# Later bank sums, silus and gate products in a hand-ordered gate-and-up loop, and one ring of transposition banks

## The chip, the cores and the metric

The kernel runs on one core of one Trainium2 chip. The metric is the device time of one execution in microseconds, as the median of several runs. One further execution was recorded by the hardware profiler; all rows below come from it.

Five engines work side by side, each through its own queue in order: TensorE (PE in the rows; PEld is its weight load), VectorE (DVE), ScalarE (ACT), GpSimd (POOL) and SyncE (SP, which here issues transfers). They wait for each other through semaphores. Matmuls write into PSUM, eight banks of 128 x 512 float32; DVE and ACT read the banks.

## The reference

A decoder trunk of two layers for 256 positions and a width of 2048, in float32. Cut to what matters here:

```
x = x + mixer(rms_norm(x))          # layer 0: retention and short convolution; layer 1: differential attention
x = x + swiglu(rms_norm(x))         # both layers

def swiglu(h, w_gate, w_up, w_down):          # 2048 -> 5632 -> 2048
    return (jax.nn.silu(h @ w_gate) * (h @ w_up)) @ w_down
```

The change touches the product of `h` with `w_gate` and `w_up` and what makes the hidden values out of it.

## The kernel before, in words

Every float32 matmul is done as three in a reduced format: each operand is split into a high part (a cast by ACT) and a low part (the operand minus the high part, by DVE), and PE multiplies high by high, low by high and high by low (L272 to L274). The low part of the weights enters only with the third.

`gate_up` (L188) makes the hidden values of one feed-forward layer. The 5632 hidden columns are 11 pairs of 512 columns, a pair being the gate columns and the up columns of the same numbers. `ffn` (L620) runs them in three parts of 4, 4 and 3 pairs; after each part `out_proj` or an equal loop multiplies the part's hidden values by the rows of `w_down`. So within the parts one pair follows another in 3 + 3 + 2 places per layer.

The gate and up products of both halves of the 256 rows share work in the manner of Strassen: the 2048 contraction rows of a pair are four chunks of 512, of the kinds 7, 8, 7, 8. In a chunk of kind 7 seven weight operands (w11, w21, t2, t3, t4, t1, w22; t1 to t4 are sums of weight blocks) are each multiplied into one bank, six matmuls each; in a chunk of kind 8 four operands go into two banks each, twelve matmuls each. An operand with its matmuls is a slot: slots 0 to 6 are the first chunk of a pair, 7 to 10 the second, 11 to 17 the third, 18 to 21 the fourth. Seven banks are summed up over the pair: b1, b2, b6 and b4 (four banks of tag `mm`), b7 (tag `tpa`), and b3 and b5, which are one tile of two banks of tag `sc` with a single buffer. In a chunk of kind 7 the operands go, in the order above, to b1, b2, b6, b7, b4, b5 and b3.

The order of the instructions in `gate_up` is written by hand (`manual_schedule`, L305). In the loop over the slots, step i first prepares slot i+3 (`prepare`: the cast on ACT, the low part on DVE at L183, and in chunks of kind 7 a helper sum on DVE behind the low parts of w11, w21 and t2, at L242, L244 and L246), then issues the matmuls of slot i, then calls `gather(i)`. High and low parts have four buffers each, so the cast of slot i+3 waits until slot i-1 is done. `gather` acts at three slots of each pair:

- at slot 14 (t3 of the third chunk) b1 is copied twice by ACT and b6 and b7 are summed with it by DVE (L284 to L287);
- at slot 19 DVE adds b2 and b4 to them, the gate values (L290, L291), and ACT applies two silus (L293);
- at slot 21, the last, DVE adds b5 twice and b3 once, the up values (L296 to L298), and multiplies gates by ups (L300, twice). The result is handed to `splits`, which transposes it on PE through a bank of `tp_tile` and splits it into high and low parts. That job advances by one step at each slot of the second chunk of the next pair: a step that does nothing, one half of the rows, the other half.

Since every engine works in order, a DVE operation issued at slot 21 stands in front of the low part that is prepared one step later.

`tp_tile` (L73) gives a bank for transpositions: in turn one of tag `tpa` and one of `tpb`, and during `gate_up` only `tpb`, since b7 holds `tpa`.

Of the kernel before, what the change touches and what calls it, by code (L numbers as in the profile page):

```python
# [9 lines left out]
F32 = mybir.dt.float32  # L10
F32R = mybir.dt.float32r
AF = mybir.ActivationFunctionType
ALU = mybir.AluOpType
# [3 lines left out]
P = 128  # L17
D = 2048
S = 256
NT = S // P  # L20
KT = D // P
NB = 512
# [13 lines left out]
def decoder_trunk(ctx: ExitStack, tc: tile.TileContext, a: dict):  # L36
    nc = tc.nc
# [27 lines left out]
    work.begin("mix0", 4)  # L65
    ctx.callback(lambda: work.close.close())

    tp_both, tp_turn = [True], [0]

    def acc_tile(name):  # L70
        return psum.tile([P, NB], F32, tag="mm", name=name, bufs=4)

    def tp_tile(name):  # L73
        tp_turn[0] ^= 1
        tag = "tpa" if tp_turn[0] and tp_both[0] else "tpb"
        return psum.tile([P, NB], F32, tag=tag, name=name, bufs=1)


    ident = cpool.tile([P, P], F32, name="ident")
# [58 lines left out]
    jobs = deque()  # L138

    def step():  # L140
        while jobs:
            try:
                next(jobs[0])
                return
            except StopIteration:
                jobs.popleft()
# [41 lines left out]
    def gate_up(layer, wg, wu, st, r, p0, p1, hi, lo):  # L188

        kinds = st.kinds
        nc_ = len(kinds)
        last7 = max(c for c, kind in enumerate(kinds) if kind == 7)
        last8 = max(c for c, kind in enumerate(kinds) if kind == 8)
        chunks = [(b, c) for b in range(p0, p1) for c in range(nc_)]
        tiles, banks, sums, begun = {}, {}, {}, set()

        def load(n):
            if n >= len(chunks):
                return
            b, c = chunks[n]
            nm = f"f{layer}{b}_{c}"
            x, y = work.raw_tile(nm + "x"), work.raw_tile(nm + "y")
            k0 = c * KD * P
            cols = slice(b * NB, (b + 1) * NB)

            def rows(w, nk):  # L210
                return w[k0 : k0 + nk * P, cols].rearrange("(k p) n -> p k n", p=P)

            nc.sync.dma_start(y, rows(wu, KD))
            nc.sync.dma_start(x, rows(wg, KD))
            if kinds[c] == 7:
                nc.gpsimd.dma_start(y[:, 0:KC], rows(wg, KC), accum_op=ALU.add)  # L216
            tiles[n] = {"w11": x[:, 0:KC], "w21": x[:, KC:KD], "w12": y[:, 0:KC], "w22": y[:, KC:KD]}

        SEVEN = (
            ("w11", (("b1", "a11"),)), ("w21", (("b2", "a12"),)), ("t2", (("b6", "s2"),)), ("t3", (("b7", "s3"),)),  # L220
            ("t4", (("b4", "a22"),)), ("t1", (("b5", "s1"),)), ("w22", (("b3", "s4"),)),
        )
        EIGHT = (
            ("w11", (("b2", "a11"), ("b4", "a21"))), ("w21", (("b2", "a12"), ("b4", "a22"))),
            ("w12", (("b5", "a21"), ("b3", "d1"))), ("w22", (("b5", "a22"), ("b3", "d2"))),
        )
        slots = []
        for n, (b, c) in enumerate(chunks):
            for operand, products in SEVEN if kinds[c] == 7 else EIGHT:
                slots.append((n, b, c, operand, products))  # L230
        ready = {}

        def prepare(i):
            n, b, c, operand, _ = slots[i]
            w = tiles[n]
            nm = f"f{layer}{b}_{c}"
            where = {"t1": "w12", "t3": "w11", "t4": "w21"}.get(operand, operand)
            ready[i] = split_w(w[where], nm + operand)
            if kinds[c] == 7:
                if operand == "w11":  # L240
                    w["t2"] = work.tile([P, KC, NB], F32, tag="t2", name=nm + "t2", bufs=1)
                    nc.vector.tensor_tensor(w["t2"], w["w12"], w["w22"], ALU.add)  # L242
                elif operand == "w21":
                    nc.vector.tensor_tensor(w["w11"], w["t2"], w["w11"], ALU.subtract)  # L244
                elif operand == "t2":
                    nc.vector.tensor_tensor(w["w21"], w["t2"], w["w21"], ALU.add)  # L246
            if operand == "w22":
                load(n + 3)

        def get_banks(b):  # L250
            nm = f"f{layer}{b}_"
            for i in (1, 2, 6, 4):
                banks[b, f"b{i}"] = acc_tile(f"{nm}p{i}")
            banks[b, "b7"] = psum.tile([P, NB], F32, tag="tpa", name=nm + "p7", bufs=1)
            b35 = psum.tile([P, 2, NB], F32, tag="sc", name=nm + "p35")
            banks[b, "b3"], banks[b, "b5"] = b35[:, 0], b35[:, 1]

        def multiply(i):
            n, b, c, operand, products = slots[i]
            whi, wlo = ready.pop(i)  # L260
            a = st.blocks(c)
            if (b, "b1") not in banks:
                get_banks(b)
            for bank, act in products:
                ahi, alo = a[act]
                acc = banks[b, bank]
                last = (last7 if bank in ("b1", "b6", "b7") else nc_ - 1) == c
                last = last and (kinds[c] == 7 or operand in ("w21", "w22"))
                for j in range(KC):
                    first = (b, bank) not in begun  # L270
                    begun.add((b, bank))
                    nc.tensor.matmul(acc, lhsT=ahi[:, j], rhs=whi[:, j], start=first, stop=False)  # L272
                    nc.tensor.matmul(acc, lhsT=alo[:, j], rhs=whi[:, j], start=False, stop=False)  # L273
                    nc.tensor.matmul(acc, lhsT=ahi[:, j], rhs=wlo[:, j], start=False, stop=last and j == KC - 1)  # L274

        def gather(i):

            n, b, c, operand, _ = slots[i]
            nm = f"f{layer}{b}"
            if c == last7 and operand == "t3":  # L280
                u = work.tile([P, NT, NB], F32, tag="u", name=nm + "u", bufs=1)
                g = work.tile([P, NT, NB], F32, tag="gs", name=nm + "gs", bufs=1)
                sums[b] = u, g
                nc.scalar.copy(u[:, 0], banks[b, "b1"])  # L284
                nc.vector.tensor_tensor(u[:, 0], banks[b, "b6"], u[:, 0], ALU.subtract)
                nc.scalar.copy(g[:, 0], banks[b, "b1"])
                nc.vector.tensor_tensor(u[:, 1], banks[b, "b7"], u[:, 0], ALU.add)  # L287
            if c == nc_ - 1 and operand == "w21":
                u, g = sums[b]
                nc.vector.tensor_tensor(g[:, 0], banks[b, "b2"], g[:, 0], ALU.add)  # L290
                nc.vector.tensor_tensor(g[:, 1], banks[b, "b4"], u[:, 1], ALU.subtract)  # L291
                for t in range(NT):
                    nc.scalar.activation(g[:, t], g[:, t], AF.Silu, scale=r[:, t : t + 1])  # L293
            if c == nc_ - 1 and operand == "w22":
                u, g = sums[b]
                nc.vector.tensor_tensor(u[:, 1], banks[b, "b5"], u[:, 1], ALU.add)  # L296
                nc.vector.tensor_tensor(u[:, 0], banks[b, "b5"], u[:, 0], ALU.add)
                nc.vector.tensor_tensor(u[:, 0], banks[b, "b3"], u[:, 0], ALU.add)  # L298
                for t in (1, 0):
                    nc.vector.scalar_tensor_tensor(  # L300
                        g[:, t], u[:, t], r[:, t : t + 1], g[:, t], op0=ALU.mult, op1=ALU.mult
                    )
                return splits((g[:, 1], g[:, 0]), hi, lo, 4 * (b - p0), f"h{layer}{b}", (1, 0))

        with tc.manual_schedule():  # L305
            for n in range(3):
                load(n)
            for i in range(AHEAD):
                prepare(i)
            for i, (n, b, c, operand, _) in enumerate(slots):  # L310
                if i + AHEAD < len(slots):
                    prepare(i + AHEAD)
                multiply(i)
                job = gather(i)
                if job:
                    jobs.append(job)
                if kinds[c] == 8 and n % nc_ == 1:
                    step()

    def act_pair(nk, tag, name):  # L320
        hi = apool.tile([P, nk, S], F32R, tag=tag + "h", name=name + "_hi")
# [156 lines left out]
            yield  # L478
            transpose4(srcs[t], dst, t, f"{name}{t}")

    def splits(srcs, hi, lo, k0, name, order=range(NT)):
        for src, t in zip(srcs, order):
            yield
            split4(src, hi, lo, k0, t, f"{name}{t}")


    st = Stream("n0", 0)
# [132 lines left out]
    def ffn(layer, st, r, after):  # L620
        wg, wu, wd = a["ffn_w_gate"][layer], a["ffn_w_up"][layer], a["ffn_w_down"][layer]
        res = None
        for part, (p0, p1) in enumerate(((0, 4), (4, 8), (8, 11))):
            hi, lo = act_pair(KT, "act", f"h{layer}{part}")
            tp_both[0] = False
            gate_up(layer, wg, wu, st, r, p0, p1, hi, lo)
            tp_both[0] = True
            nk, row0 = 4 * (p1 - p0), p0 * NB
            if part < 2:
                out_proj(f"d{layer}{part}", wd, nk, hi, lo, 0, row0, stream=False)  # L630
# [15 lines left out]
    st, r = ffn(0, st, r, 16)  # L646
# [28 lines left out]
    for i in range(2):  # L675
        ct, sn = rtab[:, 2 * i], rtab[:, 2 * i + 1]
        g = gains[:, i]
# [190 lines left out]
```

## Time and profile before

| | |
|---|---|
| median of 3 runs | 2257.22 us (2255.91 to 2258.88) |
| the profiled execution | 2256.58 us, span 2254.8 us |
| mean granted TensorE clock | 0.994 of full speed |
| PE busy | 2195.8 us, 97% |
| DVE busy | 1628.6 us, 72% |
| ACT busy | 1151.4 us, 51% |
| POOL busy | 174.1 us, 8% |
| moved by DMA | 441.99 MB, 196 GB/s |

How to read the rows. The busy line gives for each engine its busy time, share of the span and number of instructions. The slices cut the span in 40; a digit is a share in tenths, 9 being 90% or more. A line of the waits reads: engine, tile and source line, what it waited for, then the total in us, the number of waits and the longest. A line of the timeline reads: start in us, duration in us, engine, source line, operation, output and input, shapes, how many in a row are merged (x2), and in brackets the time that the engine stood idle before it and what released it. A line of the windows reads: the stretch in us from the start of the span, its length, the busy time and instructions of each engine, the mean granted clock (PEclk), the busy share of the DMA engines and what they moved. Matmuls overlap in their pipeline: they last 0.39 us in the rows but start every 0.23 us.

### The profile page before, as it was taken

To read this page: it belongs to the slowest core of one execution; us is meant where nothing else is said; L and a number is where in the kernel's file an instruction comes from. 1 tells how busy PE (TensorE), PEld (TensorE's weight loads), DVE (VectorE), ACT (ScalarE), POOL (GpSimd) and SP (SyncE) were. 2 spreads that over 40 slices of the span, in tenths; PEclk is the share of its full clock that TensorE was granted. 3 is DMA by queue.
4 is the path that set the end of the run, shared out by engine and by line. 5 is a ranking of instruction groups with operands and counts; after the bars stand their busy time and mean duration, and the time that the engine had idled before them with its cause. 6 is when DMAs were issued, how large, how long until landed. Compare 5 with 4: busy or idle time off the path is not lost. (4 is left out here: it accounts for less than half of the span.)

```text
span 2254.8 us, 25858 instructions
## 1 busy us (share of the span) xinstructions
PE 2195.8 (97%) x9851; PEld 1801.7 (80%) x9851; DVE 1628.6 (72%) x1742; ACT 1151.4 (51%) x1362; POOL 174.1 (8%) x148
## 2 busy tenths in 40 slices
PE   9999999999999999999999999998999999999999
PEld 7888888777887778878888888787778877788777
DVE  5555567888568885787577787677885688857884
ACT  5444455555346553555555544455564455545552
POOL 1100000000000000000132233000000000000000
PEclk9999999999999999999999999999999999999999
DMA  8555566666577656766465555466665767656752
GB/s 284 171 182 187 187 224 193 199 188 222 189 212 213 207 205 197 222 178 224 139 195 167 185 168 187 168 183 204 200 203 200 223 192 227 198 193 210 213 206 94
DMA packets 224832, 441.99 MB, mean 196 GB/s; under 512 B 8044, under 2 KB 11588, under 8 KB 224580
## 3 DMA queue, kind: packets, MB, share of 16 engines
q1 hardware_dynamic: 209904, 414.34, 54.0%
q0 software_dynamic: 11968, 23.07, 6.4%
q10 hardware_dynamic: 2836, 2.93, 0.4%
q8 instruction: 77, 1.26, 0.2%
q14 instruction: 47, 0.39, 0.1%
HBM read 438.22 MB, written 2.10 MB: 195 GB/s over the span
## 5 line engine op out<-in xcount | busy, mean ns | idle before, releaser
L216 POOL DMA_DIRECT2D f_0y<-in_ffn_w_gate_dram x22 | 26.6, 1210 | 1034.3 <-issue 214.3
L272 PE MATMUL f_p<-f_1w_hi,n_hi 128*128 128x512 f32 x264 | 106.2, 402 | 0.0
L274 PE MATMUL f_p<-f_3w_lo,n_hi 128*128 128x512 f32 x264 | 103.7, 393 | 0.4 <-DVE f_3w_lo L183 0.4
L274 PE MATMUL f_p<-f_1w_lo,n_hi 128*128 128x512 f32 x264 | 103.6, 392 | 0.0
L273 PE MATMUL f_p<-f_3w_hi,n_lo 128*128 128x512 f32 x264 | 103.2, 391 | 0.0
L273 PE MATMUL f_p<-f_1w_hi,n_lo 128*128 128x512 f32 x264 | 103.0, 390 | 0.0
L272 PE MATMUL f_p<-f_3w_hi,n_hi 128*128 128x512 f32 x264 | 103.0, 390 | 0.0
L183 DVE TENSOR_TENSOR f_0w_lo<-f_0x,f_0w_hi 128x1024 fp32r<-128x1024 f32 x44 | 53.9, 1226 | 56.6 <-ACT f_0w_hi L181 56.4
L274 PE MATMUL f_p<-f_0t_lo,n_c_sh 128*128 128x512 f32 x132 | 55.5, 420 | 40.1 <-DVE f_0t_lo L183 40.1
L183 DVE TENSOR_TENSOR f_2w_lo<-f_2x,f_2w_hi 128x1024 fp32r<-128x1024 f32 x44 | 53.9, 1226 | 35.5 <-ACT f_2w_hi L181 35.5
L181 ACT CAST f_0t_hi<-f_0x 128x1024 fp32r<-128x1024 f32 x44 | 46.2, 1051 | 56.3 <-DVE f_0x L244 25.2
L181 ACT CAST f_1w_hi<-f_1x 128x1024 fp32r<-128x1024 f32 x44 | 46.2, 1050 | 53.3 <-PE f_p L273 53.3
L181 ACT CAST f_0w_hi<-f_0x 128x1024 fp32r<-128x1024 f32 x44 | 45.9, 1043 | 47.9 <-PE f_p L273 27.9
L181 ACT CAST f_2w_hi<-f_2x 128x1024 fp32r<-128x1024 f32 x44 | 46.2, 1050 | 44.2 <-PE f_p L273 32.3
L274 PEld LDWEIGHTS f_p<-f_0t_lo,n_c_sh 128*128 128x128 f32 x132 | 25.9, 196 | 52.8 <-DVE f_0t_lo L183 47.1
L166 DVE TENSOR_TENSOR d00o_lo<-d00o_raw,d00o_hi 128x1024 fp32r<-128x1024 f32 x32 | 39.2, 1226 | 38.3 <-ACT d00o_hi L164 38.3
L166 DVE TENSOR_TENSOR d11o_lo<-d11o_raw,d11o_hi 128x1024 fp32r<-128x1024 f32 x32 | 39.2, 1225 | 38.3 <-ACT d11o_hi L164 38.3
L166 DVE TENSOR_TENSOR d01o_lo<-d01o_raw,d01o_hi 128x1024 fp32r<-128x1024 f32 x32 | 39.2, 1225 | 38.3 <-ACT d01o_hi L164 38.3
L166 DVE TENSOR_TENSOR d10o_lo<-d10o_raw,d10o_hi 128x1024 fp32r<-128x1024 f32 x32 | 39.2, 1225 | 38.3 <-ACT d10o_hi L164 38.3
L181 ACT CAST f_2t_hi<-f_2x 128x1024 fp32r<-128x1024 f32 x44 | 46.3, 1051 | 35.6 <-PE f_p L273 25.2
L166 DVE TENSOR_TENSOR n1o_lo<-n1o_raw,n1o_hi 128x1024 fp32r<-128x1024 f32 x32 | 39.1, 1224 | 30.0 <-ACT n1o_hi L164 30.0
L164 ACT CAST d11o_hi<-d11o_raw 128x1024 fp32r<-128x1024 f32 x32 | 33.6, 1049 | 52.3 <-PE d11o_a L173 46.7
(710 smaller groups left out, 7310.7 us busy)
## 6 DMA issues: line engine op xcount, KB each, us to landing
f_0y<-in_ffn_w_up_dram SPq DMA_DIRECT2D x22, 1024.0 KB, 6.4
f_0x<-in_ffn_w_gate_dram SPq DMA_DIRECT2D x22, 1024.0 KB, 6.6
f_1y<-in_ffn_w_up_dram SPq DMA_DIRECT2D x22, 1024.0 KB, 5.2
f_1x<-in_ffn_w_gate_dram SPq DMA_DIRECT2D x22, 1024.0 KB, 5.2
f_2y<-in_ffn_w_up_dram SPq DMA_DIRECT2D x22, 1024.0 KB, 5.3
f_2x<-in_ffn_w_gate_dram SPq DMA_DIRECT2D x22, 1024.0 KB, 6.0
f_3y<-in_ffn_w_up_dram SPq DMA_DIRECT2D x22, 1024.0 KB, 5.2
f_3x<-in_ffn_w_gate_dram SPq DMA_DIRECT2D x22, 1024.0 KB, 6.1
```

The source lines that it names most:

```text
L164: nc.scalar.copy(whi, part)
L166: nc.vector.tensor_tensor(wlo, part, whi.bitcast(F32), ALU.subtract)
L181: nc.scalar.copy(whi, src)
L183: nc.vector.tensor_tensor(wlo, src, whi.bitcast(F32), ALU.subtract)
L216: nc.gpsimd.dma_start(y[:, 0:KC], rows(wg, KC), accum_op=ALU.add)
L272: nc.tensor.matmul(acc, lhsT=ahi[:, j], rhs=whi[:, j], start=first, stop=False)
L273: nc.tensor.matmul(acc, lhsT=alo[:, j], rhs=whi[:, j], start=False, stop=False)
L274: nc.tensor.matmul(acc, lhsT=ahi[:, j], rhs=wlo[:, j], start=False, stop=last and j == KC - 1)
```

## The change

The sums, copies, silus and products of `gather` are put into a table, `later`, under the slot after whose matmuls they are to be issued, and the loop issues them there; what is still in the table behind the last slot of a part is issued at once, in the same order. The copies of b1 go from slot 14 to 16, the sums of b6 and b7 from 14 to 18, the silus from 19 to 22 (slot 0 of the next pair), the sums of b5 and b3 from 21 to 24 (slot 2 of the next pair), the products from 21 to 29 (slot 7 of the next pair), and with them the hand-over to `splits`. The sums of b2 and b4 stay at 19. The two halves of the rows are multiplied and transposed in the order 0, 1 instead of 1, 0. `tp_tile` draws from one tag of two buffers everywhere, and b7 is drawn from it too.

```diff
-    tp_both, tp_turn = [True], [0]
     def tp_tile(name):
-        tp_turn[0] ^= 1
-        tag = "tpa" if tp_turn[0] and tp_both[0] else "tpb"
-        return psum.tile([P, NB], F32, tag=tag, name=name, bufs=1)
+        return psum.tile([P, NB], F32, tag="tp", name=name, bufs=2)
...
-            banks[b, "b7"] = psum.tile([P, NB], F32, tag="tpa", name=nm + "p7", bufs=1)
+            banks[b, "b7"] = tp_tile(nm + "p7")
...
+            def at(k, f):
+                later.setdefault(i + k, []).append(f)
             if c == last7 and operand == "t3":
...
-                nc.scalar.copy(u[:, 0], banks[b, "b1"])
-                nc.vector.tensor_tensor(u[:, 0], banks[b, "b6"], u[:, 0], ALU.subtract)
-                nc.scalar.copy(g[:, 0], banks[b, "b1"])
-                nc.vector.tensor_tensor(u[:, 1], banks[b, "b7"], u[:, 0], ALU.add)
+                def copies():
+                    nc.scalar.copy(u[:, 0], banks[b, "b1"])
+                    nc.scalar.copy(g[:, 0], banks[b, "b1"])
+                def inner():
+                    nc.vector.tensor_tensor(u[:, 0], banks[b, "b6"], u[:, 0], ALU.subtract)
+                    nc.vector.tensor_tensor(u[:, 1], banks[b, "b7"], u[:, 0], ALU.add)
+                at(2, copies)
+                at(4, inner)
             if c == nc_ - 1 and operand == "w21":
...
+                at(0, gates)
+                at(3, silu)
             if c == nc_ - 1 and operand == "w22":
...
-                for t in (1, 0):
-                    nc.vector.scalar_tensor_tensor(
-                        g[:, t], u[:, t], r[:, t : t + 1], g[:, t], op0=ALU.mult, op1=ALU.mult
-                    )
-                return splits((g[:, 1], g[:, 0]), hi, lo, 4 * (b - p0), f"h{layer}{b}", (1, 0))
+                def hidden():
+                    for t in range(NT):
+                        nc.vector.scalar_tensor_tensor(
+                            g[:, t], u[:, t], r[:, t : t + 1], g[:, t], op0=ALU.mult, op1=ALU.mult
+                        )
+                    jobs.append(splits((g[:, 0], g[:, 1]), hi, lo, 4 * (b - p0), f"h{layer}{b}"))
+                at(3, ups)
+                at(8, hidden)
...
                 multiply(i)
-                job = gather(i)
-                if job:
-                    jobs.append(job)
+                gather(i)
+                for f in later.pop(i, ()):
+                    f()
                 if kinds[c] == 8 and n % nc_ == 1:
                     step()
+            for i in sorted(later):
+                for f in later[i]:
+                    f()
```

`gates`, `silu` and `ups` hold the lines that stood there before.

## Rows read from the trace of the kernel before

**Rows 1.** The page, busy time of each engine, and the clock by slices.

```profile
PE 2195.8 (97%) x9851; PEld 1801.7 (80%) x9851; DVE 1628.6 (72%) x1742; ACT 1151.4 (51%) x1362; POOL 174.1 (8%) x148
...
PEclk9999999999999999999999999999999999999999
```

**Rows 2.** The waits of PE over the whole span, largest first.

```profile
PE f_p L274 <- DVE f_0t_lo L183: 40.1, 16, 3.8
PE n_tp L358 <- DMA x_sb<-in_x_dram: 5.3, 2, 4.6
PE on_tp L329 <- DVE on L789: 3.0, 1, 3.0
```

**Rows 3.** The timeline of PE: one boundary, and four single waits.

```profile
411.20 0.50 PE L274 MATMUL f_p<-f_2t_lo,n_c_sh 128*128 128x512 f32 x1 [0.60 <-DVE f_2t_lo L183]
...
474.31 0.39 PE L272 MATMUL f_p<-f_0w_hi,n_hi 128*128 128x512 f32 x1
...
477.04 0.41 PE L272 MATMUL f_p<-f_0t_hi,n_c_sh 128*128 128x512 f32 x1
...
478.44 0.40 PE L272 MATMUL f_p<-f_0t_hi,n_c_sh 128*128 128x512 f32 x1
...
481.49 0.51 PE L274 MATMUL f_p<-f_0t_lo,n_c_sh 128*128 128x512 f32 x1 [2.42 <-DVE f_0t_lo L183]
...
528.05 0.50 PE L274 MATMUL f_p<-f_0t_lo,n_c_sh 128*128 128x512 f32 x1 [2.42 <-DVE f_0t_lo L183]
...
1568.00 0.79 PE L274 MATMUL f_p<-f_0t_lo,n_c_sh 128*128 128x512 f32 x1 [3.75 <-DVE f_0t_lo L183]
```

**Rows 4.** Windows of 6 us, PE alone, behind three waits.

```profile
408.94:414.94 6.00, 5.40 (x22) 1.00 0.20 38
481.49:487.49 6.00, 6.00 (x19) 0.72 0.65 210
528.05:534.05 6.00, 6.00 (x26) 1.00 0.61 209
```

**Rows 5.** Windows of two whole pairs, from slot 0 to the next slot 0.

```profile
474.31:520.87 46.56, 44.14 (x189) 35.70 (x188) 39.76 (x40) 25.75 (x28) 2.39 (x2) 0.96 0.66 200
520.87:565.88 45.01, 42.59 (x190) 34.58 (x188) 39.03 (x39) 25.87 (x28) 0.00 (x0) 1.00 0.60 206
```

**Rows 6.** A window on the first chunk of a pair (PE, PEld, DVE, ACT, POOL).

```profile
474.31:484.00 9.69, 7.27 (x29) 5.62 (x28) 9.65 (x12) 5.04 (x5) 0.00 (x0) 0.92 0.09 12
```

**Rows 7.** The timeline of DVE around the same boundary.

```profile
470.00 0.68 DVE L291 TENSOR_TENSOR f01gs<-f_p,f01u 128x512 f32<-128x512 f32 x1
472.42 1.23 DVE L183 TENSOR_TENSOR f_0w_lo<-f_0x,f_0w_hi 128x1024 fp32r<-128x1024 f32 x1 [1.75 <-ACT f_0w_hi L181]
473.56 1.22 DVE L244 TENSOR_TENSOR f_0x<-f_0t,f_0x 128x1024 f32<-128x1024 f32 x1
...
476.97 0.69 DVE L296 TENSOR_TENSOR f01u<-f_p,f01u 128x512 f32<-128x512 f32 x1
477.57 0.68 DVE L297 TENSOR_TENSOR f01u<-f_p,f01u 128x512 f32<-128x512 f32 x1
478.29 0.69 DVE L298 TENSOR_TENSOR f01u<-f_p,f01u 128x512 f32<-128x512 f32 x1
478.89 1.40 DVE L300 SCALAR_TENSOR_TENSOR f01gs<-f01u,n_r,f01gs 128x512 f32<-128x512 f32 x2
480.22 2.35 DVE L183 TENSOR_TENSOR f_0t_lo<-f_0x,f_0t_hi 128x1024 fp32r<-128x1024 f32 x2
```

**Rows 8.** The timeline of ACT there, and its table load in layer 1.

```profile
470.11 1.34 ACT L293 ACTIVATE f01gs<-f01gs,n_r 128x512 f32<-128x512 f32 x2 [3.03 <-DVE f01gs L290]
471.36 1.03 ACT L181 CAST f_0w_hi<-f_0x 128x1024 fp32r<-128x1024 f32 x1
...
474.89 1.05 ACT L181 CAST f_0t_hi<-f_0x 128x1024 fp32r<-128x1024 f32 x1 [1.56 <-DVE f_0x L244]
...
1555.33 1.28 ACT L293 ACT_TABLE_LOAD   x1 [3.07 <-DVE f10gs L290]
```

More of the change, by code (lines that the diff above doesn't have):

```diff
@@ L274, in multiply @@
                     nc.tensor.matmul(acc, lhsT=ahi[:, j], rhs=wlo[:, j], start=False, stop=last and j == KC - 1)
+        later = {}
         def gather(i):
@@ L288, in gather, with gates @@
+                at(2, copies)
+                at(4, inner)
             if c == nc_ - 1 and operand == "w21":
                 u, g = sums[b]
[L290 to L293, printed above, removed]
+                def gates():
+                    nc.vector.tensor_tensor(g[:, 0], banks[b, "b2"], g[:, 0], ALU.add)
+                    nc.vector.tensor_tensor(g[:, 1], banks[b, "b4"], u[:, 1], ALU.subtract)
@@ L294, in gather, with silu @@
+                def silu():
+                    for t in range(NT):
+                        nc.scalar.activation(g[:, t], g[:, t], AF.Silu, scale=r[:, t : t + 1])
+                at(0, gates)
+                at(3, silu)
             if c == nc_ - 1 and operand == "w22":
                 u, g = sums[b]
-                nc.vector.tensor_tensor(u[:, 1], banks[b, "b5"], u[:, 1], ALU.add)
-                nc.vector.tensor_tensor(u[:, 0], banks[b, "b5"], u[:, 0], ALU.add)
-                nc.vector.tensor_tensor(u[:, 0], banks[b, "b3"], u[:, 0], ALU.add)
@@ L299, in gather, with ups @@
-                for t in (1, 0):
-                    nc.vector.scalar_tensor_tensor(
-                        g[:, t], u[:, t], r[:, t : t + 1], g[:, t], op0=ALU.mult, op1=ALU.mult
-                    )
-                return splits((g[:, 1], g[:, 0]), hi, lo, 4 * (b - p0), f"h{layer}{b}", (1, 0))
+                def ups():
+                    nc.vector.tensor_tensor(u[:, 1], banks[b, "b5"], u[:, 1], ALU.add)
+                    nc.vector.tensor_tensor(u[:, 0], banks[b, "b5"], u[:, 0], ALU.add)
+                    nc.vector.tensor_tensor(u[:, 0], banks[b, "b3"], u[:, 0], ALU.add)
@@ L305, in gate_up @@
+                def hidden():
+                    for t in range(NT):
+                        nc.vector.scalar_tensor_tensor(
[4 more added lines that the diff above has]
+                at(8, hidden)
         with tc.manual_schedule():
@@ L479, in transposes, with splits @@
             transpose4(srcs[t], dst, t, f"{name}{t}")
-    def splits(srcs, hi, lo, k0, name, order=range(NT)):
-        for src, t in zip(srcs, order):
+    def splits(srcs, hi, lo, k0, name):
+        for t in range(NT):
             yield
-            split4(src, hi, lo, k0, t, f"{name}{t}")
+            split4(srcs[t], hi, lo, k0, t, f"{name}{t}")
     st = Stream("n0", 0)
@@ L624, in ffn @@
             hi, lo = act_pair(KT, "act", f"h{layer}{part}")
-            tp_both[0] = False
             gate_up(layer, wg, wu, st, r, p0, p1, hi, lo)
-            tp_both[0] = True
             nk, row0 = 4 * (p1 - p0), p0 * NB
```

## Prediction

> **What bounds the kernel now.** I read the busy shares first. TensorE (PE) is busy 97% of the span and its granted clock is near full in every slice [rows 1], so time can only be won where PE stands still or runs at the low clock. The list of PE's waits says where: 40.1 us in 16 waits of one kind, the third matmul of an operand whose low part VectorE (DVE) has not yet written [rows 2]. Nothing else on PE's list is above 5.3 us, and the largest wait on a transposition bank or what fills it is 3.0 us [rows 2]. Sixteen is the number of places where one gate-and-up pair follows another: 3 + 3 + 2 per layer, two layers.
>
> The timeline of PE shows one of them. I number the 22 operands ("slots") of a pair 0 to 21 and mark those of the next pair with a prime. Slot 0' starts at 474.31, 2' at 477.04 (so 1.37 us a slot) and 3' (t3) at 478.44; its third matmul waits 2.42 us and starts at 481.49 [rows 3]. Fourteen of the sixteen waits are exactly this long; one is 2.48, and the first of layer 1 is 3.75 [rows 3]. Then the clock: in the 6 us after the wait at 481.49 the mean granted clock is 0.72, so PE runs partly at 1.2 GHz, while after the equally long wait at 528.05 it is 1.00 (2.4 GHz throughout) [rows 4]. Read that way, 6 of the 16 waits are followed by 0.72 to 0.75 and 10 by 1.00. Whole pairs give the price: 46.56 us with a wait and the low clock, 45.01 us with the wait alone [rows 5], so the low clock costs 1.55 us. What hangs on these waits is 40.1 + 6 x 1.55 = 49.4 us. A pair without either would take 45.01 - 2.42 = 42.59 us.
>
> Why DVE is late: in the ten us of the next pair's first chunk DVE is busy 9.65 of 9.69 us [rows 6]. Its queue [rows 7] shows two causes. First, after slot 21 ends (474.31) it owes the previous pair five operations, three sums at 476.97 to 478.89 and two gate products to 480.22, in front of the low part of slot 3', which starts only at 480.22. Secondly, earlier it idles 1.75 us before 472.42, waiting for a cast of ScalarE (ACT). ACT's rows [rows 8] show why: ACT was held 3.03 us by the silus, which wait for DVE's gate sums, and the cast stood behind them until 471.36.
>
> **The change, part by part.** No operation is added or removed and none of the moved steps issues a DMA, so SP's and POOL's queues hold what they held. In DVE's queue the sums of banks b6 and b7 go from behind slot 17's low part to behind slot 21's; the three sums of b5 and b3 from behind slot 2' to behind slot 5'; the two products from there to behind slot 10'. On ACT the copies of b1 go past two casts and the silus from behind the cast of slot 0' to behind that of slot 3'.
>
> I walk the queues of this boundary with the spacings of the rows: large DVE operations follow each other every 1.14 us and last 1.22, the bank sums follow at 0.60, 0.72 and 0.60 and last 0.69 [rows 7]; a cast lasts 1.05, and a pair of silus holds ACT for 1.25 [rows 8]; the cast of slot i+3 cannot begin before slot i starts (four weight buffers). The sums of b6 and b7 now fall where DVE waited for casts, and DVE reaches slot 0' 0.1 us later than before: nothing. The gate sums stay (469.5 to 470.7), but the cast of 1' no longer stands behind the silus: DVE goes straight on, and is through with slot 2' and its helper sum at 475.3 instead of 476.97. The cast of 3' takes 474.31 to 475.36 and its low part is written by 476.6; PE wants it at 478.90, so the wait of 2.42 us goes, with 2.3 us to spare. Then the silus: ACT 475.3 to 476.5, the cast of 4' behind them until 477.56, its low part at 477.59 (DVE idles 1.0 us), that of 5' at 478.73, both over 1.5 us early. Next the three sums: 479.87, 480.47, 481.19, ending at 481.88. Low part of 6': 481.79 to 483.01, wanted at 483.10. That is 0.1 us of margin: zero cost by the walk, no more.
>
> **What is late next** is the pair of banks b3 and b5. Slot 5' (t1) is the first to write b5 and would start at 478.44 + 1.40 + 1.37 = 481.21. Both banks are one tile with one buffer. If PE waits for the tile's last reader, it starts at 481.88 + 0.05 = 481.93 and loses 0.7 us; if for the last reader of bank b5 alone, the second sum ends at 481.16 and the loss is nil. Before, the sums were done at 478.97, over 2 us ahead, so no row tells which holds. I take 0.7: the allocation is of the tile, and PE then has one wait for it. The first pair of layer 1 has in addition an activation table load of 1.28 us in front of its silus [rows 8], which delays casts, low parts and sums alike: 2.0 us there, or 1.3 for bank b5 alone. A gap of 0.7 us should leave the clock alone: after a gap of 0.60 us, at 411.20, the granted clock stayed at 1.00 [rows 3, 4]. Below zero I see no room, because the 49.4 us are already all that these boundaries lose.
>
> The two products now stand behind the low part of slot 10'. The low parts of 6' to 10' follow each other from 481.79, so the products run from 481.79 + 5 x 1.14 = 487.49 to 488.9. The transpositions that read them stand in PE's queue behind slot 8'. With the 0.7 us lost, 6' starts at 483.33, 7' at 484.70, and 7' and 8' have twice the matmuls, 2.75 us each: 8' ends near 490.2. So 1.3 us of slot 8' covers the products; without that cover PE itself would wait, as the transpositions are in its own queue. In this second chunk DVE has one or two operations of 1.14 us for each 2.75 us of PE, which hides the products' 1.33 us. At the end of a part the late steps run at once, in the order they had: nothing.
>
> The **ring of transposition banks** keeps two banks. Within a part b7 holds one and transpositions share the other, as now. Elsewhere it may let a transposition take whichever bank is free instead of the one whose turn it is; the most it can win is near the 3.0 us wait [rows 2], and one such wait is also what it could add. I take 0, with 3 us either way.
>
> **The sum**, against the profiled execution of 2256.6 us (span 2254.8): 2256.6 - 49.4 + 15 x 0.7 + 2.0 = 2219.7. The median of the runs is 0.6 us above the profiled one: 2220 us. A difference within 0.2%, some 4.5 us, cannot be told from no change.
>
> The Trainium skill (Perfetto Trace Analysis, Optimization Strategy) says that the same gap repeating on the engine that should be saturated can mean that there is no SBUF or PSUM free for the next tile. The rows name DVE's low part of t3 as releaser of the gap, a datum and not a buffer, so the trace so far does not bear it out; by that rule the change would hold banks longer and lose, which is the last rival below.
>
> **Rivals.** (1) *PE waits for bank b5 alone.* Then 2256.6 - 49.4 + 1.3, with the median's 0.6: 2209. For it: the sums read bank by bank. Against: one tile, one buffer. (2) *DVE becomes the bound.* A pair holds 39.0 to 39.8 us of DVE work [rows 5] against 42.59 us, leaving room for 2.8 us of idling, where it now idles 6.0 (45.01 - 39.03). My walk finds about 2.7: 1.0 before 4', 0.7 in the fourth chunk's long slots and the rest around the transpositions. If it is 4 to 5, a pair takes 43.8 to 44.8 and the time is 2256.6 - 49.4 + 16 x (1.2 to 2.2) = 2226 to 2242. (3) *The gap only changes its operand*: DVE goes on idling 6.0 us in a pair, and the time stays within 0.2% of 2257. Against: 1.75 us of the idling is one cast behind the silus, and that is removed. (4) *Slower: the wait for the banks grows.* Its place is slot 5', where PE now stands behind five links in a row, silus, cast, low part, low part, sums, any of which can slip. The 16 boundaries lose 49.4 us now, 3.1 each. Counting low clocks as often as today (0.6 us each), the time is above today's by over 0.2% once the wait passes 2.8 us, that is, once the sums end 2.1 us later than in my walk. At 3.5 us: 2256.6 + 16 x (4.1 - 3.1) = 2273. Against: the longest single thing known to slip is the table load of 1.28 us, and it occurs once.
>
> **Chances**: forecast (2213 to 2230) 0.50, (1) 0.22, (2) 0.13, (3) 0.06, (4) 0.09. Faster 0.50 + 0.22 + 0.13 = 0.85, same 0.06, slower 0.09. The range takes in (1) less the ring's 3 us and most of (2): 2205 to 2240, leaving out some 0.18.
>
> **What would show it.** Right: the waits on f_0t_lo are gone from PE's list; in their place 16 waits of about 0.7 us at the first matmul of t1 (slot 5'), released by the sum of b3; pairs of 43.3 us at clock 1.00; the cast of 1' right after slot 19, the silus behind the cast of 3'. Rival 1 shows no PE wait at all and pairs of 42.6. Rival 2 shows PE waiting for low parts of 6' or of the third chunk. Wrong altogether if the transpositions of the previous pair's products wait for DVE, or if waits under 1 us are followed by the low clock.

## The result and the profile after

| | before | after |
|---|---|---|
| median of the runs | 2258.05 us (4 runs, 2255.91 to 2261.51) | 2217.28 us (4 runs, 2216.31 to 2219.25) |
| ratio to before | 1 | 0.9819, 95% interval 0.9802 to 0.9836 |
| profiled execution | 2256.58 us, span 2254.8 | 2216.82 us, span 2215.0 |
| mean granted clock | 0.994 | 0.998 |
| PE busy | 97% | 99% |

The kernel became 40.8 us faster by the medians; the forecast was 2220 us, the range 2205 to 2240. DVE's busy time did not fall (1632.2 us after 1628.6): no work went, only its order changed.

The waits of PE after, three kinds out of the list (columns as in [rows 2]):

```profile
PE on_tp L356 <- DVE on L814: 2.5, 2, 1.9
...
PE f_p L268 <- DVE f10u L317: 2.0, 1, 2.0
...
PE f_p L268 <- DVE f00u L317: 0.6, 1, 0.6
```

The 40.1 us of waits for f_0t_lo [rows 2] are gone. In their place stands a wait at each of the sixteen boundaries, one line for each, since the tile's name has the pair's number: fifteen of 0.62 us like f00u, and one of 2.0 at the first boundary of layer 1. All are released by L317 of the new kernel, the sum of b3, third of the three. The wait at the transpositions of the attention is split in two and hardly shorter.

The timeline of DVE after, at the boundary that answers [rows 7]:

```profile
466.35 0.68 DVE L303 TENSOR_TENSOR f01gs<-f_p,f01u 128x512 f32<-128x512 f32 x1
466.94 1.22 DVE L179 TENSOR_TENSOR f_0w_lo<-f_0x,f_0w_hi 128x1024 fp32r<-128x1024 f32 x1
...
470.35 1.22 DVE L242 TENSOR_TENSOR f_0x<-f_0t,f_0x 128x1024 f32<-128x1024 f32 x1
471.75 1.23 DVE L179 TENSOR_TENSOR f_0t_lo<-f_0x,f_0t_hi 128x1024 fp32r<-128x1024 f32 x1 [0.19 <-ACT f_0t_hi L177]
473.92 1.23 DVE L179 TENSOR_TENSOR f_0t_lo<-f_0x,f_0t_hi 128x1024 fp32r<-128x1024 f32 x1 [0.94 <-ACT f_0t_hi L177]
475.07 1.22 DVE L179 TENSOR_TENSOR f_0t_lo<-f_0y,f_0t_hi 128x1024 fp32r<-128x1024 f32 x1
...
477.52 0.69 DVE L317 TENSOR_TENSOR f01u<-f_p,f01u 128x512 f32<-128x512 f32 x1
...
483.80 1.41 DVE L321 SCALAR_TENSOR_TENSOR f01gs<-f01u,n_r,f01gs 128x512 f32<-128x512 f32 x2
```

This pair starts at 470.66. The low part of 1' (466.94) follows the gate sums with no gap; the 1.75 us of [rows 7] are gone. The low part of 3' starts at 471.75, 1.1 us behind the pair's start, where it had been 5.9 us behind (480.22 against 474.31). DVE now idles 0.94 us before the low part of 4', because ACT applies the silus:

```profile
470.67 1.05 ACT L177 CAST f_0t_hi<-f_0x 128x1024 fp32r<-128x1024 f32 x1 [1.71 <-PE f_p L269]
471.63 1.33 ACT L307 ACTIVATE f01gs<-f01gs,n_r 128x512 f32<-128x512 f32 x2
472.86 1.03 ACT L177 CAST f_0t_hi<-f_0x 128x1024 fp32r<-128x1024 f32 x1
```

And PE's timeline, first matmul of t1 and the first transposition of the products:

```profile
478.36 0.47 PE L268 MATMUL f_p<-f_0t_hi,n_c_sh 128*128 128x512 f32 x1 [0.62 <-DVE f01u L317]
...
486.71 0.60 PE L356 MATMUL h_tp<-ident,f01gs 128*128 128x128 f32 x4
```

The third sum ends at 478.21 and PE writes b5 from 478.36. The products end at 485.2 and the transpositions start without a wait at 486.71, so slot 8' covers them by 1.5 us (1.3 in the prediction). Windows on this pair, and on the 6 us behind its wait (all five engines, columns as in [rows 5, 6]):

```profile
470.66:513.87 43.21, 42.59 (x190) 34.54 (x189) 39.75 (x40) 25.84 (x28) 2.39 (x2) 1.00 0.69 214
478.36:484.36 6.00, 6.00 (x26) 4.91 (x27) 6.00 (x6) 2.73 (x4) 0.00 (x0) 1.00 0.87 301
```

A pair takes 43.2 us instead of 45.0 or 46.6 [rows 5], and the clock stays at 2.4 GHz behind the wait.

### The profile page after: what moved, and what is told of

The parts are those of the page before. It is cut to its first block, busy times and chain, and to the rows that moved or that the text cites. A ratio compares the mean times of both kernels' runs of the same rounds, so it can differ in the third digit from the quotient of the medians.

```text
span 2215.0 us, 25885 instructions
## 1 busy us (share of the span) xinstructions
PE 2185.2 (99%) x9851; PEld 1794.0 (81%) x9851; DVE 1632.2 (74%) x1742; ACT 1153.4 (52%) x1362; POOL 172.6 (8%) x148
## 5 line engine op out<-in xcount | busy, mean ns | idle before, releaser
L179 DVE TENSOR_TENSOR f_0t_lo<-f_0x,f_0t_hi 128x1024 fp32r<-128x1024 f32 x44 | 53.3, 1224 | 19.2 <-ACT f_0t_hi L177 19.2
L177 ACT CAST f_0t_hi<-f_0x 128x1024 fp32r<-128x1024 f32 x44 | 45.9, 1043 | 39.3 <-PE f_p L269 25.7
L179 DVE TENSOR_TENSOR f_2w_lo<-f_2x,f_2w_hi 128x1024 fp32r<-128x1024 f32 x44 | 53.8, 1224 | 15.4 <-ACT f_2w_hi L177 15.4
L268 PE MATMUL f_p<-f_0t_hi,n_c_sh 128*128 128x512 f32 x132 | 53.4, 405 | 11.3 <-DVE f10u L317 2.0
L179 DVE TENSOR_TENSOR f_3w_lo<-f_3y,f_3w_hi 128x1024 fp32r<-128x1024 f32 x44 | 51.9, 1222 | 13.8 <-PE f_p L270 13.8
L179 DVE TENSOR_TENSOR f_0w_lo<-f_0x,f_0w_hi 128x1024 fp32r<-128x1024 f32 x44 | 53.8, 1222 | 11.1 <-ACT f_0w_hi L177 11.1
L177 ACT CAST f_1w_hi<-f_1y 128x1024 fp32r<-128x1024 f32 x44 | 46.2, 1051 | 29.9 <-PE f_p L269 29.9
```

The lines of the kernel that those rows point to most:

```text
L177: nc.scalar.copy(whi, src)
L179: nc.vector.tensor_tensor(wlo, src, whi.bitcast(F32), ALU.subtract)
```

## The experiments

Each ratio is to the kernel before as it ran beside that kernel; its median there lay between 2257.6 and 2258.1 us. A "boundary pair" is a pair that follows another within a part, sixteen in all. "Lost" is the sum over these sixteen and the first pair of each layer of what they take above the same pairs of the fastest kernel, where a boundary pair takes 42.36 us. The column before it gives the usual length; in most of the kernels the first boundary pair of layer 1 is longer.

| kernel | median us | ratio to before (95%) | boundary pair us | lost us |
|---|---|---|---|---|
| before | 2258.05 | 1 | 45.01, low clock 46.56 | 53.8 |
| ring only | 2257.29 | 0.9999 (0.9990 to 1.0009) | 45.01, low clock 46.6 | 52.6 |
| silus only | 2216.84 | 0.9816 (0.9802 to 0.9831) | 43.17 | 14.0 |
| after | 2217.28 | 0.9819 (0.9802 to 0.9836) | 43.18 | 14.5 |
| after, two tags | 2218.03 | 0.9821 (0.9805 to 0.9838) | 43.17 | 15.9 |
| after, b6 and b7 back | 2218.26 | 0.9824 (0.9808 to 0.9841) | 43.17 | 15.4 |
| after, products alone stay moved | 2226.79 | 0.9860 (0.9844 to 0.9876) | 43.68 | 23.5 |
| after, silus back | 2227.82 | 0.9866 (0.9851 to 0.9880) | 43.85 | 25.7 |
| after, third sum one step later | 2236.30 | 0.9904 (0.9884 to 0.9923) | 44.22 | 32.4 |
| after, sums behind 1' | 2208.68 | 0.9780 (0.9764 to 0.9796) | 42.65 | 6.1 |
| after, sums behind 0' | 2202.81 | 0.9754 (0.9740 to 0.9769) | 42.36 | 0 |
| after, sums back at slot 21 | 2203.05 | 0.9754 (0.9740 to 0.9769) | 42.36 | 0 |

The fastest kernel's profiled execution took 2202.9 us. That plus the lost time gives each other profiled execution within 1.3 us: 2256.7 for before (measured 2256.6), 2217.4 for after (2216.8), 2235.3 for the third sum later (2235.7). So these pairs account for the difference between the kernels, to within 1.3 us.

### The ring alone, and all but the ring

```diff
-    tp_both, tp_turn = [True], [0]
...
-        tp_turn[0] ^= 1
-        tag = "tpa" if tp_turn[0] and tp_both[0] else "tpb"
-        return psum.tile([P, NB], F32, tag=tag, name=name, bufs=1)
+        return psum.tile([P, NB], F32, tag="tp", name=name, bufs=2)
...
-            banks[b, "b7"] = psum.tile([P, NB], F32, tag="tpa", name=nm + "p7", bufs=1)
+            banks[b, "b7"] = tp_tile(nm + "p7")
...
-            tp_both[0] = False
...
-            tp_both[0] = True
```

The first kernel is before with this edit, the second is after with this edit reversed.

> The kernel before with the ring of two transposition banks alone; every step of gather stays at its old slot. Theory (the gain is the sixteen gaps, the ring moves nothing): 2257 us, within 3 us, sixteen waits on f_0t_lo of 2.42 us and some low clock, as before. Rival (the ring carries a part of the gain, by freeing a bank for the transpositions): 2250 us or less and other waits at the transpositions.

> The changed kernel with the ring undone: two tags of one transposition bank each in turn, as before, and the bank of b7 of tag tpa. Theory (the ring is neutral): 2217 us within 3, sixteen waits of 0.62 us at the banks of b5 and b3. Rival (the moved steps need the ring): above 2222 us, with waits at the transpositions of the products.

Measured: 2257.29 and 2218.03 us. The waits of PE of the ring alone:

```profile
PE f_p L270 <- DVE f_0t_lo L179: 40.1, 16, 3.8
...
PE on_tp L325 <- DVE on L783: 2.8, 2, 2.2
```

The sixteen waits stand as in [rows 2]. The ring moves nothing that can be measured, in either surrounding.

### The silus alone

```diff
+        later = {}
...
-                for t in range(NT):
-                    nc.scalar.activation(g[:, t], g[:, t], AF.Silu, scale=r[:, t : t + 1])
+                def silu():
+                    for t in range(NT):
+                        nc.scalar.activation(g[:, t], g[:, t], AF.Silu, scale=r[:, t : t + 1])
+                later.setdefault(i + 2, []).append(silu)
...
+                for f in later.pop(i, ()):
+                    f()
                 job = gather(i)
```

> The kernel before with the silus alone moved, from slot 19 to the end of slot 21, ahead of the products that read them. Theory: the cast of slot 1' no longer stands behind the silus, DVE loses its idle 1.75 us there and reaches the low part of 3' at 478.43 on the clock of the old boundary instead of 480.22. It is written by 479.70 and wanted at 478.90: a gap of 0.8 us in place of 2.42 at all sixteen places, and no low clock, so 2205.5 (the changed kernel less its 11.3 us of waits) + 16 x 0.8 = 2218 us. Rival (the five operations of DVE in front of 3' are the cause and the silus only sit in an idle stretch): gaps stay near 2.4 us, 2250 us or more.

Measured: 2216.84 us. DVE's timeline and the one wait of PE at a boundary whose pair starts at 470.75:

```profile
470.44 1.22 DVE L246 TENSOR_TENSOR f_0x<-f_0t,f_0x 128x1024 f32<-128x1024 f32 x1
471.57 0.69 DVE L302 TENSOR_TENSOR f01u<-f_p,f01u 128x512 f32<-128x512 f32 x1
...
474.82 2.36 DVE L183 TENSOR_TENSOR f_0t_lo<-f_0x,f_0t_hi 128x1024 fp32r<-128x1024 f32 x2
```

```profile
476.09 0.50 PE L274 MATMUL f_p<-f_0t_lo,n_c_sh 128*128 128x512 f32 x1 [0.58 <-DVE f_0t_lo L183]
```

The five operations of DVE still stand in front of the low part of 3', yet the gap is 0.58 us instead of 2.42 (0.81 us lost by the pair's length, 43.17 against 42.36; 0.8 expected): DVE begins them 0.8 us after the pair's start instead of 2.7. Two silus moved two slots give the same time as the whole change. That the two times agree is chance: here PE still waits 0.58 us for the low part of 3', after the whole change 0.62 us for the banks. The rival, that the silus sit in an idle stretch and do not matter, is out.

### All but the silus, and the products alone

The first kernel is after with the silus back at slot 19:

```diff
-                at(3, silu)
+                at(0, silu)
```

The second is after with only the products still moved:

```diff
-                at(2, copies)
-                at(4, inner)
+                at(0, copies)
+                at(0, inner)
...
-                at(3, silu)
+                at(0, silu)
...
-                at(3, ups)
+                at(0, ups)
```

> The changed kernel with the silus back at slot 19; all else stays moved. Theory: DVE idles 1.75 us again before the low part of 1', the gap at 3' is still gone (low part written by 478.2, wanted at 478.9 on the old boundary's clock), but the sums of b5 and b3 end at 482.5 instead of 481.9, so the wait of PE for the two banks grows from 0.62 to 1.4 us, 2.6 in the first pair of layer 1: 2205.5 + 15 x 1.4 + 2.6 = 2229 us. Rival (silus irrelevant): waits of 0.62 and 2217 us, as the changed kernel.

> The changed kernel with the copies, the sums of b6 and b7, the silus and the sums of b5 and b3 back at their old slots; only the two products stay at slot 7'. Theory (each gap is what stands in DVE's queue before the low part of 3'): two operations of 0.66 us less in front of it, so the low part is written 1.3 us after PE wants it instead of 2.6: about 2202.3 (the changed kernel less 14.5 us that its boundaries lose against pairs of 42.36 us) + 15 x 1.3 + 2.6 = 2224 us, more by 1.55 us for each gap that the low clock follows. Rival (the products cost nothing where they stood, since DVE stood waiting for the cast anyway): gaps of 2.4 us, 2250 us or more.

Measured: 2227.82 and 2226.79 us. PE's wait at one boundary of each:

```profile
479.18 0.47 PE L268 MATMUL f_p<-f_0t_hi,n_c_sh 128*128 128x512 f32 x1 [1.29 <-DVE f01u L317]
```

```profile
477.59 0.50 PE L270 MATMUL f_p<-f_0t_lo,n_c_sh 128*128 128x512 f32 x1 [1.09 <-DVE f_0t_lo L179]
```

Both waits are near the size that the walk along DVE's queue gave. With the silus early PE waits 1.29 us for the banks by the row and loses 1.49 us by the pair's length (1.4 expected). With only the products moved, two operations less stand in front of 3'; the gap is 1.09 us by the row and 1.32 us by the pair's length (1.3 expected). No low clock follows any of these gaps, the longest of them 2.4 us. So moving the products is worth some 31 us by itself, moving the silus some 41, and the two are not added: both shorten the same gap.

### Which reader the banks wait for

```diff
                     nc.vector.tensor_tensor(u[:, 0], banks[b, "b5"], u[:, 0], ALU.add)
+                def ups3():
                     nc.vector.tensor_tensor(u[:, 0], banks[b, "b3"], u[:, 0], ALU.add)
...
                 at(3, ups)
+                at(4, ups3)
```

> The changed kernel with the third of the three sums, that of b3, one step later than the two of b5: behind the low part of 6' instead of in front of it. Theory (PE's first matmul into b5 waits for the last reader of the tile of both banks): that wait grows with the third sum by about 1.1 us, to 1.6 us of idle time, 2202.3 + 16 x 1.8 + 1.3 = 2232 us. Rival (it waits for the readers of b5 alone): the wait before b5 goes, one of 0.2 to 0.4 us comes at the first matmul into b3 a slot later, about 2209 us.

Measured: 2236.30 us. DVE and PE:

```profile
477.65 0.68 DVE L316 TENSOR_TENSOR f01u<-f_p,f01u 128x512 f32<-128x512 f32 x1
...
479.38 0.69 DVE L319 TENSOR_TENSOR f01u<-f_p,f01u 128x512 f32<-128x512 f32 x1
```

```profile
480.21 0.47 PE L268 MATMUL f_p<-f_0t_hi,n_c_sh 128*128 128x512 f32 x1 [1.62 <-DVE f01u L319]
```

The last reader of b5 ends at 478.33; PE's first matmul into b5 waits until 480.21, behind the sum of b3 that ends at 480.07. The tile of both banks is given back as a whole. The time is 4 us above the expectation. Some 2.3 of them are traced: a pair loses 1.86 us where 1.8 was reckoned, and in the first boundary pair of layer 1 (46.93 us) the low clock came on top, behind a gap of 2.96 us.

### Where the sums may stand

Three kernels differ from after in one number: the sums behind slot 1', behind 0', and back at slot 21.

```diff
-                at(3, ups)
+                at(2, ups)
```

(`at(1, ups)` and `at(0, ups)` in the other two.)

> The changed kernel with the three sums issued behind slot 1', one step sooner than in the changed kernel and one later than in the kernel with the sums behind slot 0'. Theory (DVE's queue is what counts, step by step): the bank wait goes, but the sums now stand in front of the low part of 5', which is written at 4.3 + 3.3 us after the pair's start against 7.36 when PE wants it: 0.2 us lost at each boundary, 2202.3 + 16 x 0.25 = 2206 us, with waits of 0.1 us or less on f_0t_lo. Rival (any place that frees the banks in time is as good): 2203 us, as with the sums behind slot 0'.

> The changed kernel with the sums of b5 and b3 issued behind slot 0' (and so behind the low part of 3') instead of behind 2'. Theory (PE's remaining 0.62 us is the reuse of the two banks, which waits for the third sum; DVE idles 0.9 us before the low part of 4', room for half of the sums): the sums end some 3 us before PE wants the banks, the low parts of 4' and 5' come 0.6 us or more ahead of need, no wait is left at the sixteen boundaries, pairs take 42.6 us: 2216.8 - 11.3 = 2205.5 us. Rival (DVE has no room there, the wait only goes to the low part of 4' or 5'): waits on f_0t_lo of 0.5 us or more and 2214 us or above.

> The changed kernel with the three sums of b5 and b3 back at slot 21, where the kernel before had them; silus, products, copies and the sums of b6 and b7 stay moved. Theory (with the cast of 1' no longer behind the silus, DVE has room for three sums in front of the low part of 3', only not for five operations): the low part of 3' is written 0.5 us before PE wants it, the banks are free long before, no wait is left: 2203 us, so that moving the sums was the one part of the change that cost time (14 us). Rival (the sums have to leave the place in front of 3'): waits of 0.5 us or more on f_0t_lo, 2211 us or above.

Measured: 2208.68, 2202.81 and 2203.05 us. A whole pair with the sums behind 0':

```profile
470.01:512.37 42.36, 42.36 (x190) 34.63 (x188) 39.75 (x40) 25.83 (x28) 2.39 (x2) 1.00 0.71 220
```

PE's busy time is the whole window. The time is 2.7 us below the expectation, which took off only the waits as the rows draw them. With the sums back at slot 21, DVE's timeline at a boundary whose pair starts at 470.08:

```profile
470.90 0.68 DVE L315 TENSOR_TENSOR f01u<-f_p,f01u 128x512 f32<-128x512 f32 x1
...
472.82 2.35 DVE L179 TENSOR_TENSOR f_0t_lo<-f_0x,f_0t_hi 128x1024 fp32r<-128x1024 f32 x2
```

The low part of 3' is written at about 474.0 and PE wants it 4.6 us after the pair's start, at 474.7: there was room for three operations in front of it, only not for five. So one step of the change, moving the three sums three slots, cost 14 us of what the silus and the products had won. Both kernels without that wait, with the sums behind 0' and at slot 21, are faster than before and after. With the sums behind 1' the banks are free in time, but the low part of 5' comes late:

```profile
476.68 0.40 PE L269 MATMUL f_p<-f_0t_hi,n_c_sl 128*128 128x512 f32 x1
477.14 0.51 PE L270 MATMUL f_p<-f_0t_lo,n_c_sh 128*128 128x512 f32 x1
```

These two start 0.46 us apart, where matmuls follow each other every 0.23; the row shows no idle time, for the earlier one is drawn 0.40 us long. 6.1 us are lost in all, 1.7 of them at the first boundary of layer 1, where 0.25 was reckoned: there PE waits 0.84 us for the banks and 0.33 us for the low part.

### The sums of b6 and b7 back

```diff
-                at(2, copies)
-                at(4, inner)
+                at(0, copies)
+                at(0, inner)
```

> The changed kernel with the copies of b1 and the sums of b6 and b7 back at slot 14. Theory (they stood and stand where DVE has room; only the first pair of each layer waits 0.24 us for the low part of the fourth chunk): 2217 to 2219 us, pairs of 43.2 us as in the changed kernel. Rival (they delay the low parts of the fourth chunk, so that DVE enters the boundary late): waits at the banks above 0.62 us and 2222 us or more.

Measured: 2218.26 us, against 2217.28. At the boundaries pairs take 43.17 us as before the edit; only the first pair of each layer is 0.5 us longer (45.64 and 45.68 where after has 45.13 and 45.17), which is too little for the times to show. At the boundaries DVE had room at the old place and at the new one.

## Why the prediction was right, and where its sizes were off

- *The bound.* Right: sixteen gaps and the low clock behind some of them. But the gap's idle time is not the time lost. Pairs of 45.01 us with a 2.42 us gap stand against 42.36 without one, so a gap costs 2.65 us, not 2.42; a pair without wait was put at 42.59. The sixteen boundaries lost 52.8 us, not 49.4, and the first pairs of the layers 1.0 more. A matmul is drawn 0.39 us long though the next can start 0.23 us behind it, so some 0.16 us of each gap lie inside the earlier matmul's row.
- *The two causes in DVE's queue.* Right, and each shown alone: the silus (2216.84 us with nothing else moved) and the operations in front of 3' (2226.79 us with only the products moved). What the prediction did not draw from its own walk: it found the low part of 3' 2.3 us early, and the three sums fill 1.92 us (476.97 to 478.89 in [rows 7]). The run with the sums back at slot 21 (2203.05 us) shows that they could have stayed there; moving them cost the 14 us.
- *What is late next.* Right in place and mechanism: PE at the first matmul into b5, held by the third sum. Its size was put at 0.7 us; the row shows 0.62, and by the pairs' length it costs 0.82 (43.18 against 42.36). The table load's boundary was put at 2.0 us and shows 1.97. That b5 and b3 come free together was a choice in the prediction; the later third sum shows it.
- *The sum.* 2219.7 us against 2216.8 for the profiled execution. Both sides were too small by the hidden part of the gaps: 49.4 instead of 52.8 us lost before, 12.5 instead of 14.5 after. In the difference the two errors partly cancel, so some of the closeness of the sum is luck. The gain, put at 36.9 us, is 38.3 at the boundaries and 1.0 in the first pairs, which comes from the later sums of b6 and b7.
- *Steps costed at nothing.* The ring, the copies and the sums of b6 and b7, and the products behind 10': each held to within 1 us, all but the last by runs of their own, the last by the transpositions that start without a wait. The new order of the two halves has no run of its own.
- *The rivals.* PE waiting for b5 alone is out. DVE as the bound is out: it holds 39.75 us of work in pairs of 42.36. The gap that only changes its operand is out by the time, though 14.5 of 53.8 us did turn into the wait for the banks. The slower rival named the right place: with the third sum a step later that wait grows to 1.62 us and the kernel is still 1% faster than before. A wait of over 2.8 us at every boundary, its deciding point, was not tried.

## What to carry to other kernels

In an order written by hand, a step is placed by what is queued behind it on each engine, not by when its own result is wanted: the result of the two silus was not wanted for long, but they held a cast, which held a low part, which held TensorE. Work that is moved out of the way should be moved no further than needed, and what its operands hold (here two PSUM banks freed together) decides how far it may go; the same three sums were free at two places, cost 6 us at a third and 14 us at a fourth. When several moves shorten one gap, test them one at a time: one of them may give all of it, and another may take some back.

## What was not expected of the hardware

- The low clock does not follow a gap of a given length every time, nor at a given place of the program. It came behind 6 of the 16 gaps of before (five of about 2.42 us and the one of 3.75; 0.72 to 0.75 granted over the 6 us that follow), and behind 5 of the 16 with the ring alone, partly at other places (four of 2.42 us and again the one of 3.75). It came once behind a gap of 1.97 us (the two-tag kernel, a pair of 46.15 us where after has 44.57 with the same gap) and once behind one of 2.96 (the third sum one step later). At the boundaries no gap of 1.85 us or less was followed by it. Each time it cost between 1.3 and 1.6 us. What decides between two equal gaps stays open.
- Idle time in PE's rows is short of the lost time by about 0.2 us for each gap, and a stop of 0.2 us does not show as idle at all; the length of a repeated unit of work, here a pair, shows it.
